# Cross-covariance attention: the output written in rows of 4 KB instead of 2 KB, with 16 output matmuls a group instead of 8

## The chip, the core and the metric

The kernel runs on one core of a Trainium2 chip. The metric is the device time of one execution, in microseconds (us). A core has a matrix engine (TensorE; the profile calls its matmuls PE and its weight loads PEld), VectorE (DVE), ScalarE (ACT), GpSimd (POOL) and SyncE, whose queue (SPq) issues nearly all transfers here. 16 DMA engines move data between HBM and the on-chip memory SBUF; matmuls write to PSUM, which only PE, DVE and ACT reach.

## The reference

Q, K and V are float32 of 8 batches x 12 heads x 512 rows x 64 columns. Attention here is over the 64 columns, not the rows:

```python
Q_norm = Q / (np.linalg.norm(Q, axis=-2, keepdims=True) + 1e-10)
K_norm = K / (np.linalg.norm(K, axis=-2, keepdims=True) + 1e-10)
attn = np.einsum('bhnd,bhne->bhde', Q_norm, K_norm)
attn = np.exp(attn - np.max(attn, axis=-1, keepdims=True))
attn = attn / (np.sum(attn, axis=-1, keepdims=True) + 1e-10)
return np.einsum('bhnd,bhde->bhne', V, attn)
```

So each of 96 heads has a 64 x 64 matrix of column products, a softmax over it, and one multiplication of V by it. Inputs are 37.7 MB, the output is 12.6 MB.

## The kernel before

**Units.** Four heads make a unit u (24 of them, `HU = 4`), two units a pair s (12, `S`), two pairs a group w (6, `W`). A tile has 128 partitions: 32 partitions for each of the four heads of a unit, and in each partition `T = 16` consecutive rows of 64 columns, 4 KB of float32.

**Stages of a pair.** `load_qk` brings Q and K (lines 180 to 184), `load_v` brings V (lines 191 and 193). `cast_qk` (line 204, DVE) makes bfloat16 of them side by side. `grams` (line 224, PE) multiplies: 64 weight loads and 64 matmuls a unit, four heads at a time in four row strips of 32 of the array; unit 23, the last (`WIDE`), takes 32 in strips of 64. `squares` (line 231) and `sums` (line 243) on DVE take the norms, `cross` copies the products of Q and K out of PSUM, `powers` and `scales_q` (lines 249 to 262, ACT) make the scales, `scale_k` (line 254, POOL) applies K's, `logits` (line 267, PE) transposes, `exps` (line 273, ACT) takes the exponentials with their sums, and `normalise` (lines 279 and 282, DVE) writes them as bfloat16 into a tile `ab`.

**V and the output.** `cast_v` (lines 167 and 169) makes bfloat16 of V, `vtrans` (line 293, PE) transposes it in pieces of 8 transposes, `vcopy` (lines 165 and 167) takes a piece to SBUF as `vt`. `outs` (line 310, PE) multiplies `vt`, as weights, with `ab`, one group x = 0 to 3 of a pair at a time: 8 weight loads and 8 matmuls, each of 64 output partitions, into a PSUM tile `po` of 128 x 512 float32, of which there are two (`ps_o`, `bufs=2`). `ocopy` (lines 165 and 167) copies a `po` to a part of a tile `so`; it has 13 buffers of 4 KB a partition. Two groups fill one `so`, and `store` (line 198) writes it: 512 KB, in HBM rows of 2 KB. The very last `so` goes in two stores of 256 KB.

**The order of work.** It is laid down before the launch. `Order` (line 22) is a planner: it holds pieces of work with an engine, a cost, what each must come after, and a rank, and deals them out on a clock of its own. Each engine then works in that fixed order. The DMA queue is one of its engines: SPq issues loads and stores in the planned order, and each issue waits for the eighth issue before it to have landed and for what its buffer needs. Rotating buffers bind the stages: Q and K are three pairs deep, V three half groups, `qkb` two units, `vt` two groups.

The planner also has a rule for PE's own instructions. It counts weight loads and matmuls, and lets the count pass 190, and each further 256, only 6.1 us after the last such passage:

```python
CHUNK, FETCH, FIRST = 256, 6.1, 190
```

Lines 342 to 345 give it the number of instructions in a piece: 128 for a unit's grams, 16 for a piece of `vtrans`, 16 for a group of `outs`.

Of the kernel before, what the change touches and what calls it, by code (L numbers as in the profile page):

```python
# [13 lines left out]
D = 64  # L14
T = 16
HU = 4
J = T // 2
LN_EXP = 6
LO, HI = slice(0, D), slice(D, 2 * D)

# [82 lines left out]
def kernel(  # L103
# [27 lines left out]
    Qw = Q.rearrange("b h (p j) d -> (b h p j d)", j=J).rearrange("(u m p x) -> u p m x", m=2, p=128, x=J * D)  # L131
    Kw = K.rearrange("b h (p j) d -> (b h p j d)", j=J).rearrange("(u m p x) -> u p m x", m=2, p=128, x=J * D)

    Of = out.rearrange("b h n d -> (b h n d)").rearrange(
        "(w r e i p x) -> w e i p r x", r=2, e=2, i=2, p=128, x=J * D)

    ctx.enter_context(tc.manual_schedule())

    NB = dict(qk=3, v=3, vb=2, qkb=2, vt=2, so=13, sm=2, ab=4)
    const = ctx.enter_context(tc.tile_pool(name="const", bufs=1))  # L140
    qp = ctx.enter_context(tc.tile_pool(name="qp", bufs=NB["qk"]))
    vp = ctx.enter_context(tc.tile_pool(name="vp", bufs=NB["v"]))
# [49 lines left out]
        else:  # L192
            nc.sync.dma_start(out=o[:, c], in_=i[:, c])

    def store(s, i, k=None):
        rows = slice(None) if k is None else slice(k * (J // 2), (k + 1) * (J // 2))
        o = Of[s // 2, s % 2, i].rearrange("p r (j d) -> p r j d", d=D)
        nc.sync.dma_start(out=o[:, :, rows], in_=so[s, i][:, :, rows])

    def cast_qk(u, x):  # L200
        s, r = divmod(u, 2)
# [83 lines left out]

    def vtrans(w, q, f):

        js = range(2 * q, 2 * q + 2) if f is None else (2 * q + f,)
        pool = ps_v if f is None else late_pool()
        ps = vps[w, q, f] = pool.tile([128, 4, len(js), 128], BF16, name="vps")  # L290
        for n, j in enumerate(js):
            for c in range(4):
                nc.tensor.transpose(ps[:, c, n, :], vb[w][:, J * c + j].rearrange("p r d -> p (r d)"), identb)  # L293

    def vcopy(eng, w, q, f):
        if w not in vt:
            vt[w] = vtp.tile([128, J, 128, 4], BF16, name="vt")
        o = vt[w][:, 2 * q:2 * q + 2] if f is None else vt[w][:, 2 * q + f:2 * q + f + 1]
        copy(eng, o, vps[w, q, f].rearrange("p c j x -> p j x c"))

    def outs(s, x):
        i, k = divmod(x, 2)
        w, half = divmod(s, 2)
        po[s, x] = ps_o.tile([128, J // 2, 2, D], F32, name="po")
        for j in range(J // 2):
            for e in range(2):
                h = 2 * i + e
                x16 = slice(16 * (4 * half + h), 16 * (4 * half + h + 1))
                v = vt[w][:, k * (J // 2) + j, x16, :].rearrange("p x c -> p (x c)")
                nc.tensor.matmul(po[s, x][e * D:(e + 1) * D, j].rearrange("p r d -> p (r d)"), v, ab[s][:, h, :])  # L310

    def ocopy(eng, s, x):
        i, k = divmod(x, 2)
        if k == 0:
            so[s, i] = sop.tile([128, 2, J, D], F32, name="so")
        o = so[s, i][:, :, k * (J // 2):(k + 1) * (J // 2)].rearrange("p r j d -> p j r d")
        copy(eng, o, po[s, x])


# [22 lines left out]
    def size(key):  # L342
        if key[0] == "gr" and key[1] >= WIDE:
            return 64
        return 8 if key[0] == "vt" and key[-1] is not None else {"gr": 128, "lg": 8, "vt": 16, "ou": 16}[key[0]]

    plan = Order(size)
    X = 1.29
# [4 lines left out]
    def v_at(v):  # L353
        return V_FROM + V_PACE * v / U

    def piece(key, engines, after, behind, rank, fn, *args):
        if key[0] in ("cv", "vc", "oc", "kq", "sc"):
            plan.add(key, engines, after, behind, rank, lambda eng: fn(eng, *args))
        else:
            plan.add(key, engines, after, behind, rank, lambda eng: fn(*args))  # L360
# [39 lines left out]
    def turns(w):  # L400
        return [(q, f) for q in range(4) for f in ((0, 1) if w == W - 1 and q >= TAIL else (None,))]
# [28 lines left out]
            piece(("vc", w, q, f), copies, [("vt", w, q, f)] + free, [("vc", w, *turns(w)[n - 1])] if n else [], R["vc"] + 0.02 * w, vcopy, w, q, f)  # L430
    for s in range(S):
        for x in range(4):
            i, k = divmod(x, 2)
            n = 4 * s + x - 2
            wait = [("oc", n // 4, n % 4)] if n >= 0 else []
            order = [("ou", s, x - 1) if x else back("ou", s, 1, 3)]
            piece(("ou", s, x), {"PE": 0.5}, [("vc", s // 2, *t) for t in turns(s // 2) if t[0] // 2 == k] + [("nm", s)] + wait, order, R["ou"] + 0.01 * s, outs, s, x)
            n = 2 * s + i - NB["so"]
            free = [("st", n // 2, n % 2)] if k == 0 and n >= 0 else []
            order = [("oc", s, x - 1) if x else back("oc", s, 1, 3)]  # L440
            piece(("oc", s, x), {"ACT": 0.6, "DVE": (0.68, BIAS["oc"])} if s >= BOTH else {"ACT": 0.6}, [("ou", s, x)] + free, order, R["oc"] + 0.01 * s, ocopy, s, x)
        for i in range(2):
            order = [("st", s, 0) if i else back("st", s, 1, 1)]
            if (s, i) == (S - 1, 1):

                piece(("sh", s, i), {"DMA": 0.67}, [("oc", s, 2)], order, v_at(2 * s + i) + ST_LAG, store, s, i, 0)
                piece(("st", s, i), {"DMA": 0.67}, [("oc", s, 3)], [("sh", s, i)], v_at(2 * s + i) + ST_LAG, store, s, i, 1)
            else:
                piece(("st", s, i), {"DMA": X}, [("oc", s, 2 * i), ("oc", s, 2 * i + 1)], order, v_at(2 * s + i) + ST_LAG, store, s, i)

    held, passed = [], False
    for (emit, eng), (_, _, key, _) in zip(plan.run(), plan.order):
# [38 lines left out]
```

## Time and profile before

| | |
|---|---|
| time, median of 3 runs | 129.83 us (129.27 to 129.84) |
| span of the profiled execution, first to last instruction | 127.34 us |
| median less that span | 2.49 us |
| PE matmuls: busy, count | 76.9 us, 2128 |
| DVE, ACT, POOL busy | 93.0, 72.5, 39.0 us |
| mean rate of all DMA over the span | 398 GB/s |
| last instruction but the end of the program: the last store's issue | 117.80 us |

The page gives the profiled execution by its span; its own time with what lies around the span is taken as the span and the 2.49 us above. A line of the timeline or of the groups reads: start and length (or busy time), engine, line of the kernel, operation, output tile <- input tiles, number of instructions; in square brackets, how long the engine stood idle before it and what ended that. "issue" there means that no wait which the profile shows ended the idle time. A row of the table by stage gives a stretch, its length, each engine's busy time in it with the number of instructions, the granted clock of PE as a share, the busy share of the DMA engines, and GB/s.

### The profile page before, as it was taken

To read this page: it belongs to the slowest core of one execution; us is meant where nothing else is said; L and a number is where in the kernel's file an instruction comes from. 1 tells how busy PE (TensorE), PEld (TensorE's weight loads), DVE (VectorE), ACT (ScalarE), POOL (GpSimd) and SP (SyncE) were. 2 spreads that over 40 slices of the span, in tenths; PEclk is the share of its full clock that TensorE was granted. 3 is DMA by queue.
4 is the path that set the end of the run, shared out by engine and by line. 5 is a ranking of instruction groups with operands and counts; after the bars stand their busy time and mean duration, and the time that the engine had idled before them with its cause. 6 is when DMAs were issued, how large, how long until landed. Compare 5 with 4: busy or idle time off the path is not lost.

```text
span 127.3 us, 4886 instructions
## 1 busy us (share of the span) xinstructions
PE 76.9 (60%) x2128; PEld 63.2 (50%) x2128; DVE 93.0 (73%) x141; ACT 72.5 (57%) x220; POOL 39.0 (31%) x40
## 2 busy tenths in 40 slices
PE   0055292695946187976982999586857895647000
PEld 0045281584736075854871767374646683535000
DVE  3443749909799959997799999996999969970000
ACT  4000430737988008878395579877564799988000
POOL 4004417120834900432074301502670663300000
PEclk9999999559996555798699599968997799995555
DMA  4999999999999999999999999999999999999993
GB/s 151 353 425 409 422 414 417 417 426 414 425 423 419 408 421 413 414 419 416 430 413 415 412 422 421 417 432 416 404 405 419 399 402 401 405 402 404 409 368 109
DMA packets 15893, 50.66 MB, mean 398 GB/s; under 512 B 1408, under 2 KB 1920, under 8 KB 14464
## 3 DMA queue, kind: packets, MB, share of 16 engines
q1 hardware_dynamic: 15584, 50.34, 98.4%
q8 instruction: 16, 0.26, 0.7%
q10 hardware_dynamic: 288, 0.02, 0.2%
q14 instruction: 5, 0.04, 0.1%
HBM read 37.77 MB, written 12.58 MB: 395 GB/s over the span
## 4 chain that ended last, share of the span: by engine, by line
DVE 45%; PE 22%; issue 9%; ACT 8%; DMA 5%; SPq 1%; POOL 1%; DVEq 0%; ACTq 0%
DVE qkb L204 21%; PE gram L224 13%; DVE scr L231 9%; DVE ab L282 6%; DMA qk<-in_K_dram 5%; PE vps L293 5%; DVE vt L167 4%; PE po L310 4%; ACT ex L273 3%; DVE n L243 2%; ACT so L165 2%; ACT vt L165 2%; DVE vb L167 2%; PE lg L267 1%; DVE so L167 1%
## 5 line engine op out<-in xcount | busy, mean ns | idle before, releaser
L224 PE MATMUL gram<-qkb 32*128 32x128 bf16 (+1 forms) x1504 | 36.5, 263 | 22.9 <-DVE qkb L204 11.6
L204 DVE CAST qkb<-qk 128x1024 bf16<-128x1024 f32 x48 | 40.6, 870 | 7.4 <-DMA qk<-in_Q_dram 4.3
L224 PEld LDWEIGHTS <-qkb 32*128 32x128 bf16 (+1 forms) x1504 | 31.1, 118 | 27.1 <-DVE qkb L204 14.0
L169 POOL TENSOR_SCALAR vb<-v 128x1024 bf16<-128x1024 f32 x19 | 23.9, 1270 | 30.3 <-DMA v<-in_V_dram 24.1
L165 ACT COPY so<-po 128x512 f32<-128x512 f32 x45 | 24.9, 594 | 5.1 <-PE po L310 4.9
L165 ACT COPY vt<-vps 128x1024 bf16<-128x1024 bf16 (+1 forms) x18 | 17.8, 987 | 17.1 <-PE vps L293 17.0
L254 POOL TENSOR_TENSOR kqs<-kq,r 64x512 f32<-64x512 f32 x12 | 13.8, 1152 | 41.3 <-issue 23.1
L293 PE MATMUL vps<-identb,vb 128*128 128x128 bf16 x192 | 18.4, 249 | 8.2 <-DVE vt L167 3.8
L310 PE MATMUL po<-ab,vt 128*64 128x128 bf16 x384 | 19.3, 239 | 6.2 <-issue 2.5
L231 DVE SCALAR_TENSOR_TENSOR scr<-gram,eye 64x512 f32<-64x512 f32 x24 | 16.5, 688 | 7.7 <-PE gram L224 7.3
L293 PEld LDWEIGHTS <-vb 128*128 128x128 bf16 x192 | 13.8, 111 | 11.5 <-issue 6.4
L310 PEld LDWEIGHTS <-vt 128*64 128x64 bf16 x384 | 13.7, 119 | 10.4 <-issue 5.1
L273 ACT ACTIVATE ex<-lg,rq 128x64 f32<-128x64 f32 x48 | 14.5, 322 | 2.8 <-PE lg L267 2.8
L165 ACT COPY kq<-gram 64x512 f32<-64x512 f32 x12 | 7.0, 581 | 14.4 <-DVE scr L231 14.2
L282 DVE TENSOR_TENSOR ab<-ex,rinv 64x256 bf16<-64x256 f32 x24 | 13.2, 552 | 0.6
L273 ACT ACTIVATION_READ_ACCUMULATOR ex<-lg,rq 128x1 f32 x48 | 10.2, 213 | 0.0
L167 DVE COPY vt<-vps 128x1024 bf16<-128x1024 bf16 (+1 forms) x8 | 7.9, 1021 | 1.2 <-PE vps L293 1.1
L267 PE MATMUL lg<-eye,kqs 64*128 64x64 f32 x48 | 6.5, 262 | 2.9 <-POOL kqs L254 2.5
L243 DVE TENSOR_REDUCE n<-scr 128x8 f32<-128x512 f32 x12 | 8.2, 680 | 0.1
L267 PEld LDWEIGHTS lg<-eye,kqs 64*128 64x128 f32 x48 | 4.6, 161 | 4.7 <-POOL kqs L254 3.0
L249 ACT ACTIVATE ln<-n 128x8 f32<-128x8 f32 x12 | 2.7, 229 | 3.3 <-DVE n L243 3.3
L279 DVE RECIPROCAL rinv<-esum 128x4 f32<-128x4 f32 x12 | 2.1, 173 | 3.2 <-ACT ex L273 3.2
(17 smaller groups left out, 17.4 us busy)
## 6 DMA issues: line engine op xcount, KB each, us to landing
out_dram<-so SPq DMA_DIRECT2D x23, 512.0 KB, 10.2
v<-in_V_dram SPq DMA_DIRECT2D x11, 1024.0 KB, 17.5
qk<-in_Q_dram SPq DMA_DIRECT2D x8, 1024.0 KB, 15.9
qk<-in_K_dram SPq DMA_DIRECT2D x8, 1024.0 KB, 18.0
qk<-in_Q_dram SPq DMA_DIRECT2D x8, 512.0 KB, 11.5
qk<-in_K_dram SPq DMA_DIRECT2D x8, 512.0 KB, 11.3
v<-in_V_dram SPq DMA_DIRECT2D x2, 512.0 KB, 10.7
out_dram<-so SPq DMA_DIRECT2D x2, 256.0 KB, 8.6
```

Of the source, the lines that this page charges most:

```text
L165: nc.scalar.copy(o, i)
L167: nc.vector.tensor_copy(o, i)
L169: nc.gpsimd.tensor_scalar(out=o, in0=i, scalar1=1.0, scalar2=0.0, op0=ALU.mult, op1=ALU.add)
L204: nc.vector.tensor_copy(qkb[u][:, :, x * D:(x + 1) * D], qk32[s][:, x, r])
L224: nc.tensor.matmul(gram[s][:, h, r, 0], x, x, start=(t == 0), stop=(t == (T if u < WIDE else J) - 1))
L231: nc.vector.scalar_tensor_tensor(out=scr[s][half], in0=gram[s][half, :, :, 0, half].rearrange("p h r d -> p (h r) d"), scalar=1e-20, in1=e ...
L254: (nc.vector if eng == "DVE" else nc.gpsimd).tensor_tensor(out=kqs[s][HI], in0=kq[s][HI], in1=r8[s][HI, :, None].to_broadcast([D, 2 * HU, ...
L267: nc.tensor.transpose(l[:, h, :], kqs[s][HI, 2 * h:2 * h + 2].rearrange("p r d -> p (r d)"), eye2[HI])
L273: nc.scalar.activation(e[:, h, :], lg[s][:, h, :], AF.Exp, scale=rq[s][:, h:h + 1], accum_out=z[:, h:h + 1])
L282: nc.vector.tensor_tensor(out=a[half, :, half], in0=e[half], in1=ri[half, :, None].to_broadcast([D, HU, D]), op=ALU.mult,)
L293: nc.tensor.transpose(ps[:, c, n, :], vb[w][:, J * c + j].rearrange("p r d -> p (r d)"), identb)
L310: nc.tensor.matmul(po[s, x][e * D:(e + 1) * D, j].rearrange("p r d -> p (r d)"), v, ab[s][:, h, :])
```

## The change

A `so` tile now holds all 16 rows of a partition for both units of a pair: 8 KB a partition, 7 buffers instead of 13. All four heads of a unit lie in the 128 partitions as they lie in HBM, so a store of one pair is 1 MB in rows of 4 KB; the last pair goes in two stores of 512 KB (rows of 2 KB). For that, a group of `outs` covers 4 of the 16 rows and all four heads: 16 weight loads of 32 columns and 16 matmuls with 32 output partitions, in four column strips of the array, where it had 8 of 64 in two strips. There are still 48 groups, each of which fills the same 128 x 512 `po`. `vt` is laid out by 16 rows with two column halves instead of 8 rows with four; a piece of `vtrans` is still 8 transposes and a copy still 1024 elements a partition. A store waits for the four copies of its pair instead of two. The planner is told of 32 instructions in a group instead of 16, 0.6 us of PE instead of 0.5, and DMA pieces of 1 MB; it lays down a new order for all engines.

```diff
--- before.py
+++ after.py
+QT = T // 4
...
-    Of = out.rearrange("b h n d -> (b h n d)").rearrange(
-        "(w r e i p x) -> w e i p r x", r=2, e=2, i=2, p=128, x=J * D)
+    Of = out.rearrange("b h (p t) d -> (b h p) (t d)", t=T).rearrange("(w r e p) x -> w e p r x", r=2, e=2, p=128)
...
-    NB = dict(qk=3, v=3, vb=2, qkb=2, vt=2, so=13, sm=2, ab=4)
+    NB = dict(qk=3, v=3, vb=2, qkb=2, vt=2, so=7, sm=2, ab=4)
...
-    def store(s, i, k=None):
-        rows = slice(None) if k is None else slice(k * (J // 2), (k + 1) * (J // 2))
-        o = Of[s // 2, s % 2, i].rearrange("p r (j d) -> p r j d", d=D)
-        nc.sync.dma_start(out=o[:, :, rows], in_=so[s, i][:, :, rows])
+    def store(s, k=None):
+        o = Of[s // 2, s % 2].rearrange("p r (j d) -> p r j d", d=D)
+        rows = slice(None) if k is None else slice(k * J, (k + 1) * J)
+        nc.sync.dma_start(out=o[:, :, rows], in_=so[s][:, :, rows])
...
-        js = range(2 * q, 2 * q + 2) if f is None else (2 * q + f,)
+        js = range(QT * q, QT * (q + 1)) if f is None else range(QT * q + QT // 2 * f, QT * q + QT // 2 * (f + 1))
         pool = ps_v if f is None else late_pool()
-        ps = vps[w, q, f] = pool.tile([128, 4, len(js), 128], BF16, name="vps")
+        ps = vps[w, q, f] = pool.tile([128, 2, len(js), 128], BF16, name="vps")
         for n, j in enumerate(js):
-            for c in range(4):
-                nc.tensor.transpose(ps[:, c, n, :], vb[w][:, J * c + j].rearrange("p r d -> p (r d)"), identb)
+            for c in range(2):
+                nc.tensor.transpose(ps[:, c, n, :], vb[w][:, T * c + j].rearrange("p r d -> p (r d)"), identb)
...
     def outs(s, x):
-        i, k = divmod(x, 2)
         w, half = divmod(s, 2)
-        po[s, x] = ps_o.tile([128, J // 2, 2, D], F32, name="po")
-        for j in range(J // 2):
-            for e in range(2):
-                h = 2 * i + e
+        po[s, x] = ps_o.tile([128, QT, 2, D], F32, name="po")
+        for j in range(QT):
+            for h in range(HU):
                 x16 = slice(16 * (4 * half + h), 16 * (4 * half + h + 1))
-                v = vt[w][:, k * (J // 2) + j, x16, :].rearrange("p x c -> p (x c)")
-                nc.tensor.matmul(po[s, x][e * D:(e + 1) * D, j].rearrange("p r d -> p (r d)"), v, ab[s][:, h, :])
+                v = vt[w][:, QT * x + j, x16, :].rearrange("p x c -> p (x c)")
+                nc.tensor.matmul(po[s, x][32 * h:32 * (h + 1), j].rearrange("p r d -> p (r d)"), v, ab[s][:, h, :],
+                                 tile_position=(0, 32 * h))
...
     def ocopy(eng, s, x):
-        i, k = divmod(x, 2)
-        if k == 0:
-            so[s, i] = sop.tile([128, 2, J, D], F32, name="so")
-        o = so[s, i][:, :, k * (J // 2):(k + 1) * (J // 2)].rearrange("p r j d -> p j r d")
+        if x == 0:
+            so[s] = sop.tile([128, 2, T, D], F32, name="so")
+        o = so[s][:, :, QT * x:QT * (x + 1)].rearrange("p r j d -> p j r d")
         copy(eng, o, po[s, x])
...
-        return 8 if key[0] == "vt" and key[-1] is not None else {"gr": 128, "lg": 8, "vt": 16, "ou": 16}[key[0]]
+        return 8 if key[0] == "vt" and key[-1] is not None else {"gr": 128, "lg": 8, "vt": 16, "ou": 32}[key[0]]
...
-            piece(("ou", s, x), {"PE": 0.5}, [("vc", s // 2, *t) for t in turns(s // 2) if t[0] // 2 == k] + [("nm", s)] + wait, order, R["ou"] + 0.01 * s, outs, s, x)
+            piece(("ou", s, x), {"PE": 0.6}, [("vc", s // 2, *t) for t in turns(s // 2) if t[0] == x] + [("nm", s)] + wait, order, R["ou"] + 0.01 * s, outs, s, x)
...
+        order = [back("st", s, 1)]
+        if s == S - 1:
+            piece(("sh", s), {"DMA": X}, [("oc", s, 1)], order, v_at(2 * s) + ST_LAG, store, s, 0)
+            piece(("st", s), {"DMA": X}, [("oc", s, 3)], [("sh", s)], v_at(2 * s + 1) + ST_LAG, store, s, 1)
+        else:
+            piece(("st", s), {"DMA": 2 * X}, [("oc", s, 3)], order, v_at(2 * s + 1) + ST_LAG, store, s)
```

More of the change, by code (lines that the diff above doesn't have):

```diff
@@ L295, in vcopy @@
     def vcopy(eng, w, q, f):
         if w not in vt:
[L297 to L298 removed]
+            vt[w] = vtp.tile([128, T, 128, 2], BF16, name="vt")
+        o = vt[w][:, QT * q:QT * (q + 1)] if f is None else vt[w][:, QT * q + QT // 2 * f:QT * q + QT // 2 * (f + 1)]
         copy(eng, o, vps[w, q, f].rearrange("p c j x -> p j x c"))
     def outs(s, x):
[L302 removed]
@@ L432 @@
         for x in range(4):
-            i, k = divmod(x, 2)
             n = 4 * s + x - 2
@@ L436 @@
             order = [("ou", s, x - 1) if x else back("ou", s, 1, 3)]
-            piece(("ou", s, x), {"PE": 0.5}, [("vc", s // 2, *t) for t in turns(s // 2) if t[0] // 2 == k] + [("nm", s)] + wait, order, R["ou"] + 0.01 * s, outs, s, x)
-            n = 2 * s + i - NB["so"]
-            free = [("st", n // 2, n % 2)] if k == 0 and n >= 0 else []
+            piece(("ou", s, x), {"PE": 0.6}, [("vc", s // 2, *t) for t in turns(s // 2) if t[0] == x] + [("nm", s)] + wait, order, R["ou"] + 0.01 * s, outs, s, x)
+            free = [("st", s - NB["so"])] if x == 0 and s >= NB["so"] else []
             order = [("oc", s, x - 1) if x else back("oc", s, 1, 3)]
             piece(("oc", s, x), {"ACT": 0.6, "DVE": (0.68, BIAS["oc"])} if s >= BOTH else {"ACT": 0.6}, [("ou", s, x)] + free, order, R["oc"] + 0.01 * s, ocopy, s, x)
[L442 to L449, printed above, removed]
+        order = [back("st", s, 1)]
[4 more added lines that the diff above has]
+            piece(("st", s), {"DMA": 2 * X}, [("oc", s, 3)], order, v_at(2 * s + 1) + ST_LAG, store, s)
     held, passed = [], False
```

## The prediction

> **What bounds the kernel now.** I read the page's slices first, then the DMA queues, PE in order of time, a table by stage, and the chain that ended last.
>
> ```profile
> PEclk9999999559996555798699599968997799995555
> DMA  4999999999999999999999999999999999999993
> ...
> q1 hardware_dynamic: 15584, 50.34, 98.4%
> q8 instruction: 16, 0.26, 0.7%
> ```
>
> The DMA engines are busy in every slice, to the end: 50.34 MB of data are the first bound. The second stands in the small row: 0.26 MB in 16 packets, 16 KB each, carry instructions. PE runs 2128 weight loads and 2128 matmuls, 4256 instructions; less the 190 of the planner's rule that is 15.9 times 256. PE's own timeline shows what those packets do:
>
> ```profile
> 59.17 0.39 PE L224 MATMUL gram<-qkb 32*128 32x128 bf16 x13 [1.26 <-issue]
> ...
> 83.13 0.35 PE L310 MATMUL po<-ab,vt 128*64 128x128 bf16 x5 [1.62 <-issue]
> ...
> 89.06 0.67 PE L224 MATMUL gram<-qkb 32*128 32x128 bf16 x33 [1.24 <-issue]
> ...
> 94.98 0.39 PE L224 MATMUL gram<-qkb 32*128 32x128 bf16 x13 [1.36 <-issue]
> ...
> 103.48 1.07 PE L224 MATMUL gram<-qkb 64*128 64x128 bf16 x32
> ...
> 107.89 0.45 PE L293 MATMUL vps<-identb,vb 128*128 128x128 bf16 x5 [0.52 <-issue]
> ```
>
> PE halts in the middle of a run of like matmuls and waits for no engine. From 83.13 to 89.06 and from there to 94.98 it runs 128 pairs of weight load and matmul each time, 256 instructions, in 5.92 us: I read this as the price of a block of instructions, which comes no sooner.
>
> ```profile
> core 0: us, PE busy (x) PEld busy (x) DVE busy (x) ACT busy (x) POOL busy (x), PEclk, DMA share, GB/s
> 9.60:59.17 49.57, 31.71 (x927) 26.33 (x928) 39.58 (x58) 27.13 (x86) 17.93 (x15) 0.79 1.02 417
> 59.17:83.13 23.96, 18.42 (x512) 15.11 (x512) 22.04 (x31) 16.72 (x48) 8.55 (x7) 0.86 1.02 419
> 83.13:107.89 24.76, 18.57 (x513) 15.15 (x513) 21.71 (x34) 18.43 (x56) 10.17 (x8) 0.86 1.04 410
> 107.89:117.80 9.91, 6.33 (x113) 4.99 (x113) 5.81 (x12) 8.92 (x32) 1.04 (x1) 0.82 1.05 404
> ```
>
> The two middle rows hold 8 blocks in 48.72 us; at 5.92 they need 47.4. PE is 75 to 77% busy there and yet has 1.3 us left: in this half its instructions limit it as closely as data limit the DMA engines.
>
> ```profile
> 116.70 1.07 ACT so L165 x2
> ...
> out_dram<-so SPq DMA_DIRECT2D x2, 256.0 KB, 8.6
> ```
>
> The last copy ends at 117.77, the last store is issued at 117.80 and lands 8.6 us later, at 126.4, because stores stand in line ahead of it; 0.9 us end the span. In an idle queue the first 512 KB load landed in 3.3 us. So some 5 us of late work would hide behind that line.
>
> **The change, part by part.**
>
> *DMA.* Bytes stay, store packets halve. In the stage with stores alone the rate is 404 GB/s (2 KB rows), in that with nearly only loads of 4 and 8 KB rows 417. At 417 the 12.58 MB take 30.2 us instead of 31.1: -1.0 us, between 0 (stores are slower as stores) and -2.0 (the page's best slices reach 432). Twelve issues fewer on SPq save nothing: it waits most of the time.
>
> *PE's matmul time.* 384 pairs are added. 64 grams in four row strips take 1.07 us at full clock, 17 ns a pair; `po`'s own rows give 29 ns (16 in 0.64 against 8 in 0.41) and, at half clock, 51 (16 in 1.06 against 8 in 0.65). So 6.5 to 20 us over the span; I take 29 ns, from the same operation, 11 us. A block's 5.92 us is 46 ns a pair, so before the last grams this lies under the wait for instructions and costs nothing; were that wait gone, PE's spare time (77% busy) would cover it.
> The Trainium skill, "TensorEngine Tiling (Array Packing)", section Instruction Overhead, gives each matmul a floor of about 60 cycles, an estimated 25 ns at 2.4 GHz, which would be 9.6 us; the grams' 17 ns are under it, so the row decides.
>
> *PE's instructions.* 768 are added, three blocks, 17.8 us of supply. What counts is how many stand ahead of the last grams, which need the last Q and K and start the last softmax. By the instruction lists the last gram is weight load 1984 before and 2220 after: 236 pairs more, 1.84 blocks, 10.9 us. Against it stand reserves: 1.3 us in the two middle rows, and in the first row 7 blocks (from weight load 95, at about 10.5, on) take 48.7 us where 41.4 would do, 7.3 us. Some 4.2 of these lie before the fifth unit's grams end, at 25.64 and 1.85 blocks after load 95 (11.0 us); their place in the list is the same in both kernels and they wait for loads, so 3.1 can be used. The last gram, at 104.55 now, comes 10.9 - 4.4 = 6.5 us later if all reserve is used, 10.9 if none. I take +7.5, 112.05: the new list nearly always has output work ready.
> The Trainium skill, "Runtime: NRT & Kernel Launch", section Instruction fetch mechanics, says that PE's instructions are fetched ahead in 16 KiB blocks of 256, and that the fetch is hidden. The block size agrees with 16 packets of 16 KB; "hidden" does not agree with the 1.24 to 1.62 us halts. By that rule this term would be 0, and the time that of the first or second rival.
>
> *The loads' order.* The last K now stands behind 41.96 MB instead of 39.34 (four stores of 1 MB instead of five of 512 KB, and both halves of the last V). At 418 GB/s that is 6.3 us: issued at 86.98 with 12.5 us to landing, it lands at 99.5 now and at 105.8 then. Cast and grams of its unit follow in about 3 us, so it allows the last gram at 109: under the 112.05, hidden by PE's wait, but near.
>
> *The tail.* From the last gram to the last copy are 13.2 us now, with 13 output groups left. The new list leaves 16, and pair 9's exponentials too. The last 8 groups start at 112.42 and are copied by 117.77, 0.67 us each: three more are +2.0. The exponentials of a pair are 1.3 us of ACT, which the copies also need: +1.3 (0 to 2.3, with DVE's 1.0 to normalise). 16 groups with 8 more pairs at 29 ns are 3.7 us, half of it beside the 0.59 us copies: +1.9 (0 to 6.5, the half-clock row for all). Sum 18.4; last copy at 130.45.
>
> *The end.* Pair 8's store needs a group that in the list follows the last grams, so DMA runs out of stores and idles: the line that now covers 8.6 us is gone. The last store, 512 KB, needs 3.3 us as in an idle queue, and 0.7 for the rest of pair 10's 1 MB, ready some 3 us before it: it lands at 134.45. With the 0.9 us after it the span is 135.35 instead of 127.34: +8.0. DMA's gain of 1.0 is not in this sum, being off the path. The median of the runs lies 2.49 us above the profiled span; I carry this over: 129.83 + 8.0 = **137.8 us**.
>
> *At nothing.* `vtrans` and `vcopy` keep 8 transposes and 1024 elements a copy (ACT 1012 ns, DVE 1225) in another order of reading; I bound that by 0.1 us a copy either way, 2.6 us over 26 copies, hidden by DVE and ACT waits. A store waits for four copies, not two, and SPq holds the next loads behind it; loads are issued 16 to 18 us before they land, which covers it. If it did not, each us of delay would reach the grams. The seven `so` buffers make pair 11's first copy wait for pair 4's store, first in line after the last K: some 15 us early.
>
> **Rivals.**
>
> *DMA stays the bound (faster).* Three more blocks fit in, because the planner plans for them, and the tail hides behind the stores. For it: DMA 9 in every slice and 5 us of cover. Against it: 1.3 us of reserve in the middle rows. Place: the last copy. It decides if that comes before about 122.5, the DMA end of 125.4 less 3 us. Time: 129.83 - 1.0 = 128.8.
>
> *The last K is the bound, not instructions.* If blocks can come faster than 5.92 us when PE needs more, the last gram is at 109. With a tail of 16.5 (2.0 and 1.3 more than now) the last copy is at 125.5, landing with 4.0 at 129.5: +3.1, 132.9. For it: 6.3 us more data ahead. Against it: two equal intervals of 5.92.
>
> *Four column strips do not run beside each other.* Then the half-clock price holds through the tail: 16 groups x 8 x 51 ns, none hidden, 6.5 instead of 1.9, and before the last grams 51 ns exceed the 46 of a block: 137.8 + 4.6 = 142.4, more with the latter. For it: the clock is at half from 115 on (last slices 5). Against it: the four row strips.
>
> **How the numbers follow.** The forecast, instructions with a longer tail, 134.5 to 143: 0.62. Last K: 0.17 (130.5 to 134.5). Column strips slow, or no reserve used, above 143: 0.10. DMA stays the bound: 0.08. No change: 0.03. The range reaches from the last-K case to the top of the forecast: 131 to 143, and holds 0.79. 0.5%, 0.65 us, is about what a measurement of this kernel tells from no change. Faster 0.08, same 0.03, slower 0.89.
>
> **What the profile after would show.** Instructions: 19 packets on the instruction queue, halts on "issue" at equal distances of about 5.9 us over the whole run, last gram near 112, DMA slices under 9 in the last 15 us, the last store landing within 5 us of its issue. Wrong if: DMA is at 9 to the end (first rival); last gram near 109 just after its cast, without halts (second); 16 `po` matmuls take over 0.9 us at full clock (third). The DMA step: a store-only stretch at about 417 GB/s.

## The result, and the profile after

| | before | after |
|---|---|---|
| median of the runs on one chip | 129.55 us (128.97 to 129.84, 4 runs) | 135.56 us (135.18 to 136.17, 4 runs) |
| ratio | | 1.0484, 95% interval 1.0436 to 1.0533 |
| span of the profiled execution | 127.34 us | 133.6 us |
| end of the last gram | 104.55 | 112.17 |
| end of the last copy of an output group | 117.77 | 128.24 |
| last store landed | 126.5 | 132.54 |

The change costs 6.3 us by the ratio. The forecast of 137.8 us is 2.2 us too high: sign, mechanism and range hold, and the size, +8.0 us, is a quarter too large. Three of the kernels in the experiments below scatter by some 5 us from run to run, so ratios leave disturbed runs out throughout.

First the page of the kernel after: the slices, the queues, two groups and the last stores.

```profile
DMA  4999999999999999999999999999999997406894
GB/s 164 333 414 414 430 411 422 412 434 407 436 414 412 421 416 427 405 427 428 416 414 421 422 408 433 421 417 416 416 414 406 416 379 308 183 39 282 359 408 175
...
q1 hardware_dynamic: 12320, 50.34, 92.3%
q8 instruction: 19, 0.31, 0.8%
...
L224 PE MATMUL gram<-qkb 32*128 32x128 bf16 (+1 forms) x1504 | 38.4, 266 | 37.4 <-issue 19.6
...
L308 PE MATMUL po<-ab,vt 128*32 128x128 bf16 x768 | 21.3, 257 | 4.3 <-DVE so L167 1.6
...
out_dram<-so SPq DMA_DIRECT2D x2, 512.0 KB, 4.3
```

After the first slice the DMA engines are at 9 up to the 33rd, and then run down over three (7, 4, 0; 39 GB/s in the slice around 119 us). Before, they were at 9 until the last slice. The instruction queue carries 19 packets of 16 KB instead of 16. The grams have the same count and nearly the same busy time as before, but they stood idle for 19.6 us on "issue", where it had been 3.9 before. 768 output matmuls are busy for 21.3 us; 384 took 19.3. The grams in the kernel before:

```profile
L224 PE MATMUL gram<-qkb 32*128 32x128 bf16 (+1 forms) x1504 | 36.5, 263 | 22.9 <-DVE qkb L204 11.6 <-DVE qk L178 6.2 <-issue 3.9
```

Next, PE in order of time in the kernel after (start, length, line, operation, count; in brackets the idle time before, and what ended it).

```profile
56.65 0.66 PE L224 MATMUL gram<-qkb 32*128 32x128 bf16 x33 [2.76 <-issue]
...
62.58 0.94 PE L224 MATMUL gram<-qkb 32*128 32x128 bf16 x53 [0.96 <-issue]
...
68.77 1.00 PE L224 MATMUL gram<-qkb 32*128 32x128 bf16 x29 [3.54 <-issue]
...
108.76 0.46 PE L224 MATMUL gram<-qkb 32*128 32x128 bf16 x19 [0.33 <-DVE qkb L204]
110.33 1.84 PE L224 MATMUL gram<-qkb 32*128 32x128 bf16 x77 [1.11 <-issue]
...
125.69 1.11 PE L308 MATMUL po<-ab,vt 128*32 128x128 bf16 x32 [0.19 <-ACT so L165]
```

The halts now run through the whole kernel. In the list of DMA packets the instruction packets start at 30.59, 36.55, 42.53 and so on to 108.06: 13 steps of 5.96 us in the mean, where I had 5.92 from two intervals. The halts vary from 0.96 to 3.54 us, because the work in between is a longer or a shorter part of 5.96. The last one falls into the middle of the last grams: 19 of unit 22 run at 108.76, as soon as DVE has cast that unit's K, and its other 45 and the 32 of unit 23 wait 1.11 us more for instructions and end at 112.17. DVE has cast the last K, unit 23's, by 109.91. Without this halt its grams, 1.07 us, could have ended near 111 (an estimate from these rows); the rest of the delay lies further ahead, in grams and casts that come late.

The table by stage shows what is left of the cover at the end (start and end, length, busy time and instructions of PE, PEld, DVE, ACT, POOL, granted clock, DMA share, GB/s).

```profile
core 0: us, PE busy (x) PEld busy (x) DVE busy (x) ACT busy (x) POOL busy (x), PEclk, DMA share, GB/s
30.60:108.10 77.50, 55.07 (x1705) 44.61 (x1699) 66.95 (x94) 45.36 (x136) 27.64 (x22) 0.76 1.02 418
108.10:118.00 9.90, 6.72 (x196) 5.48 (x199) 9.71 (x17) 7.35 (x30) 1.83 (x2) 0.88 0.60 242
118.00:128.30 10.30, 7.32 (x216) 5.15 (x208) 4.27 (x12) 9.34 (x29) 0.25 (x1) 0.67 0.68 275
128.30:133.60 5.30, 0.00 (x0) 0.00 (x0) 0.00 (x0) 0.00 (x0) 0.00 (x0) 0.50 0.67 261
```

For 77.5 us PE is busy 71% of the time and DMA is full at 418 GB/s: two limits at once. From 108 on DMA runs at 60 to 68% because stores wait for copies (those of pairs 7 and 8 are issued at 111.30 and 119.12), and DVE is busy 9.71 of 9.90 us. The last copy ends at 128.24; before, stores stood in line for 8.6 us behind it, now the last one lands 4.3 us after its issue.

In spans: last gram +7.62 us, from there to the last copy 16.07 instead of 13.22 (+2.85), from the last copy to the end 5.36 instead of 9.57 (-4.21). The sum is the 6.26 us between the spans.

### The profile page after: what moved, and what is told of

Read it like the earlier page. It is cut to its first block, busy times and chain, and to the rows that moved or that the text cites. A ratio compares the mean times of both kernels' runs of the same rounds, so it can differ in the third digit from the quotient of the medians.

```text
span 133.6 us, 5626 instructions
## 1 busy us (share of the span) xinstructions
PE 83.3 (62%) x2512; PEld 67.2 (50%) x2512; DVE 98.0 (73%) x147; ACT 69.9 (52%) x215; POOL 37.9 (28%) x39
## 3 DMA queue, kind: packets, MB, share of 16 engines
q1 hardware_dynamic: 12320, 50.34, 92.3%
HBM read 37.77 MB, written 12.58 MB: 377 GB/s over the span
## 4 chain that ended last, share of the span: by engine, by line
PE 38%; DVE 24%; issue 14%; DMA 11%; ACT 8%; ACTq 0%
PE gram L224 19%; PE vps L293 11%; DVE qkb L204 10%; DMA qk<-in_K_dram 8%; DVE scr L231 7%; PE po L308 7%; ACT so L165 3%; DVE ab L282 3%; ACT ex L273 3%; DMA first<-in_Q_dram 3%; PE lg L267 2%; DVE vt L167 2%; DVE so L167 2%; ACT vt L165 1%; DVE n L243 1%
## 5 line engine op out<-in xcount | busy, mean ns | idle before, releaser
L224 PE MATMUL gram<-qkb 32*128 32x128 bf16 (+1 forms) x1504 | 38.4, 266 | 37.4 <-issue 19.6
L165 ACT COPY vt<-vps 128x1024 bf16<-128x1024 bf16 (+1 forms) x16 | 15.8, 988 | 24.8 <-PE vps L293 24.7
L165 ACT COPY so<-po 128x512 f32<-128x512 f32 x42 | 23.5, 597 | 6.2 <-PE po L308 6.1
L308 PE MATMUL po<-ab,vt 128*32 128x128 bf16 x768 | 21.3, 257 | 4.3 <-DVE so L167 1.6
L231 DVE SCALAR_TENSOR_TENSOR scr<-gram,eye 64x512 f32<-64x512 f32 x24 | 16.5, 688 | 9.5 <-PE gram L224 9.3
L293 PE MATMUL vps<-identb,vb 128*128 128x128 bf16 x192 | 20.6, 272 | 2.3 <-POOL vb L169 1.2
L308 PEld LDWEIGHTS <-vt 128*32 128x32 bf16 x768 | 14.6, 111 | 9.3 <-issue 6.2
L293 PEld LDWEIGHTS <-vb 128*128 128x128 bf16 x192 | 15.6, 122 | 5.7 <-issue 2.4
L282 DVE TENSOR_TENSOR ab<-ex,rinv 64x256 bf16<-64x256 f32 x24 | 11.9, 495 | 0.6
L167 DVE COPY vt<-vps 128x1024 bf16<-128x1024 bf16 (+1 forms) x10 | 10.4, 1060 | 0.1
L167 DVE CAST vb<-v 128x1024 bf16<-128x1024 f32 x6 | 5.5, 912 | 2.1 <-DMA v<-in_V_dram 2.1
```

The costliest lines, as they stand in the source:

```text
L165: nc.scalar.copy(o, i)
L167: nc.vector.tensor_copy(o, i)
L224: nc.tensor.matmul(gram[s][:, h, r, 0], x, x, start=(t == 0), stop=(t == (T if u < WIDE else J) - 1))
L231: nc.vector.scalar_tensor_tensor(out=scr[s][half], in0=gram[s][half, :, :, 0, half].rearrange("p h r d -> p (h r) d"), scalar=1e-20, in1=e ...
L282: nc.vector.tensor_tensor(out=a[half, :, half], in0=e[half], in1=ri[half, :, None].to_broadcast([D, HU, D]), op=ALU.mult,)
L293: nc.tensor.transpose(ps[:, c, n, :], vb[w][:, T * c + j].rearrange("p r d -> p (r d)"), identb)
```

## The experiments

**1. The split of the output matmuls alone.** The kernel before, with each output matmul of 64 columns cut in two of 32 in four column strips; groups, order, `vt`, stores and the planner stay.

```diff
-                x16 = slice(16 * (4 * half + h), 16 * (4 * half + h + 1))
-                v = vt[w][:, k * (J // 2) + j, x16, :].rearrange("p x c -> p (x c)")
-                nc.tensor.matmul(po[s, x][e * D:(e + 1) * D, j]..., v, ab[s][:, h, :])
+                for z in range(2):
+                    x8 = slice(16 * (4 * half + h) + 8 * z, 16 * (4 * half + h) + 8 * (z + 1))
+                    v = vt[w][:, k * (J // 2) + j, x8, :].rearrange("p x c -> p (x c)")
+                    q = 32 * (2 * e + z)
+                    nc.tensor.matmul(po[s, x][q:q + 32, j]..., v, ab[s][:, h, :], tile_position=(0, q))
```

> The kernel before with one part of the change: each output matmul of 64 columns is cut into two of 32 in four column strips, 16 pairs a group instead of 8. Layout, stores and the order of all work stay as before. Theory (PE's instructions come in blocks of 256, one per 5.9 us while the DMA engines are busy): 19 instruction packets instead of 16; the last gram moves from weight load 1984 to 2264, 2.19 blocks or 13.0 us, less 4.4 us of reserve: it ends near 113 instead of 104.6, the last copy is near 126, time 132.5 to 134.5. Rival 'loads' order' (the late last K is what costs): the loads are untouched, so no change, 129.6 within 0.7. Rival 'matmul time' (four column strips run one after the other): 16 po matmuls take over 0.9 us at full clock instead of about 0.45.

Measured: 134.29 us (133.41 to 134.84), ratio 1.0404 (1.0344 to 1.0463), which is 5.2 us over its 129.14. PE in order of time in this kernel:

```profile
103.16 0.39 PE L224 MATMUL gram<-qkb 32*128 32x128 bf16 x13 [1.38 <-issue]
...
109.08 1.01 PE L224 MATMUL gram<-qkb 32*128 32x128 bf16 x57 [0.68 <-issue]
...
110.58 1.07 PE L224 MATMUL gram<-qkb 64*128 64x128 bf16 x32
...
115.00 0.29 PE L293 MATMUL vps<-identb,vb 128*128 128x128 bf16 x1 [2.86 <-issue]
```

The last gram ends at 111.65, halts stand 5.92 us apart, and one of 2.86 us falls into the tail. The last K landed as early as in the kernel before, near 99. So 768 more instructions, with order, loads and stores as they were, make most of the loss.

**2. The larger unit of storing alone.** The kernel before with its matmuls of 64 columns, in which the planner has a pair's store come after all four copies, as two transfers of 512 KB in rows of 2 KB.

```diff
-    NB = dict(qk=3, v=3, vb=2, qkb=2, vt=2, so=13, sm=2, ab=4)
+    NB = dict(qk=3, v=3, vb=2, qkb=2, vt=2, so=7, sm=2, ab=4)
...
-    def store(s, i, k=None):
...
+    def store(s, k=None):
...
+        for n in (0, 1) if k is None else (k,):
+            nc.sync.dma_start(out=o[:, n], in_=i[:, n])
...
+            piece(("st", s), {"DMA": 2 * X}, [("oc", s, 3)], order, v_at(2 * s + 1) + ST_LAG, store, s)
```

> The kernel before with the other part of the change: a pair is stored when all four of its groups are copied (two stores of 512 KB issued together, rows still 2 KB; the last pair in two steps), with the planner's DMA pieces of the changed kernel. Output matmuls stay at 8 a group, 2128 pairs, 16 instruction packets. Eight stores of 512 KB now stand before the last K instead of five, and the last V after it: 40.9 MB instead of 39.3, so it lands some 3.8 us later, near 103. Theory (instruction blocks): the last gram is near 106.5, the last copy near 120, stores still stand in line then, time 129.5 to 131. Rival 'loads' order': most of the loss is here, 132.5 or more.

Four runs gave 128.84, 130.84, 131.31 and 132.55, too far apart for a verdict, so the same kernel ran again in more rounds.

> The kernel before with its matmuls of 64 columns, in which a pair's output is stored when all four groups are copied, as two stores of 512 KB in rows of 2 KB together, in the planned order of the larger stores; the same kernel as the run whose times spread from 128.84 to 132.55. Theory (the larger unit of storing is a small part of the loss, the instructions are the large one): median 129 to 131 us, at most a third of the 6.3 us. Rival (half or more of the loss): over 132 us.

Measured: median 130.70 (128.98 to 133.85, 12 runs), ratio 1.0066 (1.0022 to 1.0109): 0.9 us. Its trace shows that this kernel did not quite do what I meant. In the tail the two stores of a pair went 1.31 us apart, because each waits only for the two copies that it reads. The third version cuts a pair's stores by unit, so that each needs all four copies.

```diff
-        for n in (0, 1) if k is None else (k,):
-            nc.sync.dma_start(out=o[:, n], in_=i[:, n])
+        if k is None:
+            for r in (0, 1):
+                nc.sync.dma_start(out=o[:, :, r], in_=i[:, :, r])
+        else:
+            nc.sync.dma_start(out=o[:, k], in_=i[:, k])
```

> As the run with the larger unit of storing alone (matmuls of 64 columns), but the two stores of a pair are cut by unit and not by pair of heads, so that each needs all four copies of its pair; 512 KB each, rows of 2 KB as before. In the run before it the first of the two stores left 1.31 us ahead of the second in the tail, as soon as its own two copies had ended (issues at 122.34, 123.66, 124.97), and the last store landed 2.70 us after its issue. Theory (waiting for four copies costs in the tail alone: pair 10's 1 MB leaves at once, 1.3 us later for its first half, so the last 512 KB finds 1.3 us more of stores ahead and lands about 4.0 after its issue, as in the kernel after with 4.3): 1.0 to 1.6 us over that run's 130.4 in its undisturbed runs, 131.2 to 132.2. Rival (the wait for four copies is free, as the prediction had it): within 0.6 us of 130.4.

Measured: median 131.16 (129.28 to 134.65, 12 runs), ratio 1.0099 (1.0059 to 1.0140): 1.3 us. The wait itself shows as expected: the last store lands 4.11 us after its issue instead of 2.70. The time does not: the medians behind the two ratios are 130.65 and, in the version before, 130.35, and the intervals of the two ratios overlap. The theory's 131.2 was too much and the rival's range holds; the wait for four copies costs at most some tenths, and these runs do not tell it from nothing. Single runs of both versions reach some 134 us, which no trace here explains.

One more thing in the second version's trace matters. PE in order of time:

```profile
108.31 1.01 PE L294 MATMUL vps<-identb,vb 128*128 128x128 bf16 x8 [2.03 <-DVE vt L167]
109.25 1.89 PE L225 MATMUL gram<-qkb 64*128 64x128 bf16 x32
```

Its last gram ends at 111.14, within half a microsecond of experiment 1, and yet its profiled span is 3.8 us shorter (128.6 against 132.4). Tail and end make the difference: 13.8 us from last gram to last copy against 15.3 (where the halt of 2.86 lies), and 2.7 us for the last store against 4.6. The expectation had put its last gram near 106.5 and its last copy near 120; they came at 111.14 and 125, so the time fell into the range for another reason than was given. Instructions are not the reason: there are 16 packets, PE does not halt on issue after 98.09, and ahead of the last grams it waits 2.03 us for a DVE copy of `vt`. In the third version the last gram ends at 108.84. So the planned order with larger stores makes the last gram late by itself, by 4.3 to 6.6 us, and the time is then about 1 us longer. A late last gram is not the loss by itself. It becomes one with a longer tail behind it, and in experiment 1 the instructions make both.

The split alone (5.2, interval 4.4 to 6.0) and the larger unit (1.3, interval 0.8 to 1.8) sum to 6.5 us; both together are 6.3.

**3. Fewer grams: is it the instructions ahead of the last gram?** The kernel after, with 12 of 16 rows summed in the grams of units 0 to 22.

```diff
-        for t in range(T if u < WIDE else J):
+        last = 3 * T // 4 if u < WIDE else J
+        for t in range(last):
...
```

> The changed kernel with a quarter of the grams left out (12 of the 16 rows of a partition are summed in units 0 to 22, so the softmax is of other numbers); the order of all work and all transfers stay. 368 pairs fewer: 2144, about as many as before the change. Theory (instruction blocks): 16 packets; the last gram waits only for the last K (landing near 106) and ends near 109 instead of 112.2; the last copy is near 125, time 131 to 133. Rival 'loads' order': the loads come as in the changed kernel and the grams were waiting for them anyway: 135.6 within 0.8.

Measured: 132.98 us (132.43 to 133.85), ratio 1.0315 (1.0265 to 1.0366). PE in order of time:

```profile
105.86 0.85 PE L225 MATMUL gram<-qkb 32*128 32x128 bf16 x48 [0.62 <-DVE qkb L204]
107.06 1.07 PE L225 MATMUL gram<-qkb 64*128 64x128 bf16 x32 [0.35 <-DVE qkb L204]
```

No halt on issue is left in this stretch. The last gram ends at 108.13, 4.0 us earlier, and now waits for DVE's cast of a last K that landed at 105.54. By the two ratios 2.2 of the 4.0 us reach the time; the tail behind the last gram is 17.2 us here, where it was 16.07. The prediction's second rival gave the last K 109 and 132.9 us. That limit exists, just behind the first.

**4. Two stores after the last K: is it the loads' order?** The kernel after, with the stores of pairs 2 and 3 issued after the last K. All engines keep their order but SPq.

```diff
+        if key in (("st", 2), ("st", 3)):
+            late_st.append(emit)
+            continue
         emit(eng)
+        if key == ("lk", S - 1, 1):
+            for put in late_st:
+                put("DMA")
```

> The changed kernel with the stores of pairs 2 and 3 issued after the last K instead of before; each engine's order of work stays. The last K stands behind 39.9 MB instead of 42.0 and lands near 101 instead of 106. Theory (instruction blocks): PE is held by its blocks, so the last gram stays near 112 and the last copy near 128; DMA has 2 MB more in line for the idle stretch near 115 to 119, but the last stores still wait for the last copies: 135.6 within 0.8. Rival 'loads' order': the last gram follows K to near 107 to 108, time 131 to 132.5.

Measured: 135.63 us (134.99 to 136.26), ratio 1.0515 (1.0468 to 1.0561): nothing gained. PE in order of time:

```profile
108.74 0.46 PE L224 MATMUL gram<-qkb 32*128 32x128 bf16 x19 [0.20 <-ACT kq L165]
110.41 1.84 PE L224 MATMUL gram<-qkb 32*128 32x128 bf16 x77 [1.21 <-issue]
```

The last K landed 4.7 us earlier, at 101.39, and the last gram still ended at 112.25 after the same halt in the same place. Alone, the order of the loads moves nothing.

**5. Both.** Experiments 3 and 4 in one kernel.

> The changed kernel with both reliefs together: a quarter of the grams left out (as in the earlier run, so the softmax is of other numbers) and the stores of pairs 2 and 3 after the last K. Alone the first gave 133.0 and the second 135.6 us. Theory (instruction blocks first, the last K second): with few enough instructions the earlier K (landing near 101) now counts: the last gram ends near 105, the last copy near 121.5, and DMA has stores in line nearly to the end: 128.5 to 130. Rival 'the longer tail alone' (what is left after the blocks is the 16 groups behind the last gram): no more than 1 us better than 133.0.

Measured: 129.50 us (129.18 to 131.19), ratio 1.0040 (1.0005 to 1.0075). PE in order of time:

```profile
104.37 1.07 PE L225 MATMUL gram<-qkb 64*128 64x128 bf16 x32 [0.35 <-DVE qkb L204]
```

The last gram ends at 105.44, 0.9 us after that of the kernel before, and of the 6.3 us 0.5 are left. Instructions hold the last gram at 112, the last K at 108; with both moved, the loss is gone. It is gone in a kernel that does less work than the kernel before; whether it goes with all work kept is experiment 6. This kernel also shows the rate of stores in rows of 4 KB: only stores ran from 101 to 112 us.

```profile
101.00:112.00 11.00, 7.16 (x203) 6.04 (x200) 10.77 (x19) 8.26 (x31) 1.43 (x2) 0.85 1.02 414
```

It is 414 GB/s, where rows of 2 KB had 404.

**6. The same with all work kept.** Units in strips of 64, as unit 23 has them, need 32 pairs instead of 64, but Q and K in rows of 2 KB. The first version did this for units 16 to 23, with late stores, and the planner planned anew.

```diff
-    WIDE = U - 1
+    WIDE = U - 8
...
-        return (0, 1) if s < ONE or s == S - 1 else (None,)
+        return (0, 1) if s < ONE or 2 * s + 1 >= WIDE else (None,)
```

> All work is kept. The changed kernel with units 16 to 23 (instead of 23 alone) loaded in rows of 2 KB and multiplied in row strips of 64, 32 pairs a unit instead of 64, and the stores of pairs 2 and 3 after the last K; the planner lays the order anew. 2288 pairs, the last gram at weight load 1988, as before the change. Theory: 18 instruction packets at most, the last gram near 105, the last copy near 121, time 128.5 to 130: the gain of the 4 KB stores (1 us) and the loss from 2 KB loads (about 0.4) nearly cancel against the kernel before. Rival 'the order of the changed kernel is worse for another reason than instructions': above 132.

Measured: 133.67 us (132.48 to 134.54), ratio 1.0324 (1.0256 to 1.0391): a miss. In the profiled execution, the longest of the four (134.54), the last K landed near 99.3, but the last gram ended at 109.84, after waiting 2.87 us for DVE's cast, which stood behind other work on DVE in the new order. The rival's "above 132" holds; that the order on DVE is the reason was not tested by itself. A version with the same edit for units 20 to 23 was also a miss.

> All work is kept. As the run with units 16 to 23 in strips of 64, but units 20 to 23 alone: 2412 pairs, the last gram at weight load 2124, 0.75 of a block less than in the changed kernel (2220) and 1.06 blocks more than with eight units (1988). Theory: the last gram is at least 13 blocks of 5.96 us after load 351 at about 25.5, plus 0.9 of a block: near 108, the last copy near 124, time 131 to 132.5, between the changed kernel and the run with eight units. Rival: no dependence on the count, equal to the run with eight units within 0.8.

It gave 137.55 us (135.64 to 138.42). Beyond what the expectation says, it left out one store of 1 MB (its queue carries 49.29 MB instead of 50.34), which I had not meant; I draw nothing from it. The next two kept the order of the kernel after on every engine and gave SPq two transfers of 512 KB in the place of one.

```diff
+    WIDE = U - 8        # U - 16 in the second
+    NARROW = U - 1      # what the planner is told
-            nc.sync.dma_start(out=qk32[s][:, x, r]..., in_=(Qw, Kw)[x][U - 1])
+            for i in (0, 1) if r is None else (r,):
+                nc.sync.dma_start(out=qk32[s][:, x, i]..., in_=(Qw, Kw)[x][4 * w + 2 * i + e])
```

> The kernel after, all its work kept, with the stores of pairs 2 and 3 issued after the last K, and units 16 to 22 as well as 23 in strips of 64 (32 pairs of weight load and matmul a unit instead of 64; Q and K of these units come in rows of 2 KB, as two transfers of 512 KB for one of 1 MB). Unlike in the run that let the planner plan anew, every engine keeps the order of the kernel after. 2288 pairs; the last gram is at weight load 1996 instead of 2220 (1984 in the kernel before). Theory (blocks of instructions and the last K each hold the last gram; both are taken away): last K lands near 101, last gram near 105.5 as in the run with a quarter of the grams left out and late stores (105.44), 129.5 to 131.0 us. Rival (the miss of the planned-anew run at 133.67 came from the strips of 64 or the 2 KB loads themselves, not from the new order on DVE): 133 to 134.5 us.

Measured: 133.82 us median, but from 130.93 to 135.70 with no ratio to be given. The lowest run lies inside the theory's range, the median inside the rival's; it settles nothing.

> As the run with units 16 to 23 in strips of 64, with units 8 to 23 in strips of 64: 2032 pairs, last gram at weight load 1740, so 1.9 blocks (some 11 us at 5.96) fewer ahead of the last gram than with units 16 to 23. Theory: with 2288 pairs the instructions are no longer the bound, the last K is; more pairs taken away bring nothing, and 8 MB more in rows of 2 KB cost up to 0.65 us (404 against 417 GB/s): 129.5 to 131.5 us, within 1 us of the run with units 16 to 23. Rival (instructions still hold the last gram there): 1.5 us or more faster than that run.

Measured: 132.16 us (131.66 to 132.86, 6 runs), ratio 1.0230 (1.0179 to 1.0280): 0.7 us over the theory's range. Against the run with units 16 to 23 it is 1.7 us below the median and 1.2 above the lowest, so that comparison, on which theory and rival were to part, stays open. PE in order of time:

```profile
104.11 2.27 PE L226 MATMUL gram<-qkb 64*128 64x128 bf16 x64 [0.62 <-DVE qkb L206]
```

No halt on issue is left near the end, and the last gram ends at 106.38, 5.8 us earlier than in the kernel after; that much of the theory holds with all work kept. Yet 3.0 of the 6.3 us of loss remain. Against experiment 5 its span is 2.5 us longer: 0.9 of it before the last gram, which DVE's cast releases, and 1.8 in the landing of the last store, 5.76 us after its issue. Most parts of that store had landed by 127.48, the last one at 129.40; an instruction packet moved from 125.13 to 126.06. That it delayed that part is read from the order of events and was not tested; in experiment 4 the last store took 5.45 us with no instruction packet beside it. So the second half of the loss with all work kept has no shown cause. None of these versions beats the kernel before.

**7. What a block of instructions costs.** PE alone, in one execution: 23 blocks of 128 pairs of weight load and matmul in a row without waits between them, except one early. From about 30 to 95 us the DMA engines carry 12 loads of 1 MB (rows of 4 KB) and then 24 stores of 512 KB (rows of 2 KB); before and after that nothing.

```diff
+    pairs(0, P0)                      # P0 = 128 * 8
+    nc.vector.tensor_copy(tiles[0][:, 0, :128], acc[:, 3, :128])
+    pairs(P0, ALL)                    # ALL = 128 * 23
+    for i in range(12):
+        nc.sync.dma_start(out=tiles[i], in_=Qr[i])
+    for i in range(24):
+        nc.sync.dma_start(out=Or[i], in_=tiles[i // 2][:, :, 512 * (i % 2):512 * (i % 2) + 512])
```

> PE alone, on constant data, nothing of the reference: 23 blocks of 128 pairs of weight load and matmul in four row strips, without any wait but one copy. For the first 8 blocks no DMA runs; then 12 loads of 1 MB (4 KB rows) and 24 stores of 512 KB (2 KB rows), about 60 us, then none again. Theory A (an instruction packet waits behind the data in its DMA engine): 128 pairs take about 3.3 us without traffic and 5.9 us with it, for 4 KB rows as for 2 KB rows. Theory B (the packet has a fixed round trip): 5.9 us throughout. Theory C (it waits behind a fixed number of packets): the stretch with 2 KB rows is shorter by about 1.5 us a block than that with 4 KB rows.

Its PE in order of time, and below it the table by stage, without and with traffic:

```profile
9.71 1.97 PE L43 MATMUL acc<-x 32*128 32x128 bf16 x128 [1.49 <-issue]
13.44 1.97 PE L43 MATMUL acc<-x 32*128 32x128 bf16 x128 [1.76 <-issue]
...
30.98 1.97 PE L43 MATMUL acc<-x 32*128 32x128 bf16 x128 [0.90 <-issue]
37.18 3.60 PE L43 MATMUL acc<-x 32*128 32x128 bf16 x128 [4.23 <-issue]
43.92 3.60 PE L43 MATMUL acc<-x 32*128 32x128 bf16 x128 [3.14 <-issue]
50.12 3.60 PE L43 MATMUL acc<-x 32*128 32x128 bf16 x128 [2.60 <-issue]
...
81.92 3.60 PE L43 MATMUL acc<-x 32*128 32x128 bf16 x128 [3.73 <-issue]
88.66 2.87 PE L43 MATMUL acc<-x 32*128 32x128 bf16 x128 [3.14 <-issue]
95.68 3.60 PE L43 MATMUL acc<-x 32*128 32x128 bf16 x128 [4.15 <-issue]
99.69 1.98 PE L43 MATMUL acc<-x 32*128 32x128 bf16 x128 [0.40 <-issue]
103.41 1.97 PE L43 MATMUL acc<-x 32*128 32x128 bf16 x128 [1.75 <-issue]
```

```profile
core 0: us, PE busy (x) PEld busy (x) DVE busy (x) POOL busy (x), PEclk, DMA share, GB/s
5.00:30.00 25.00, 14.72 (x955) 13.42 (x944) 0.29 (x1) 0.00 (x0) 1.00 0.05 7
35.00:60.00 25.00, 14.41 (x512) 13.61 (x512) 0.00 (x0) 0.00 (x0) 0.50 1.03 409
65.00:85.00 20.00, 10.38 (x420) 9.81 (x411) 0.00 (x0) 0.00 (x0) 0.67 1.05 403
```

A block starts every 3.45 to 3.73 us with the DMA engines empty, every 6.2 to 6.7 under loads, every 6.2 to 7.0 under stores, and again every 3.5 to 3.7 when they are done. So theory B falls, and C too, since rows of 2 KB are no quicker; A's two levels are there, both somewhat higher than it said. The packet itself takes 0.9 to 1.2 us in either case, and a block starts 2.2 to 2.7 us after its packet does (7.38 to 9.71, 34.81 to 37.18); so nearly all of the 2.7 us more lie ahead of the packet. That it waits there behind data is the reading that fits; the trace does not show where it waits. The half clock under traffic does not explain it. The block at 30.98 runs at full clock (1.97 us), and with the loads under way the next comes only 6.20 us later; the block at 95.68 runs at half clock (3.60 us), the traffic over, and the next comes 4.01 us later. The kernel after shows the same on its own: packets 5.96 us apart while DMA is full, and, as it runs down, at 113.24 and 116.47, 5.18 and 3.23 us after the one before; in the last of these steps the DMA engines are 55% busy. So the rival with faster blocks falls before 108 us, where DMA is full, and blocks hurt the tail there little: the one that starts at 115.53 comes just as PE gets a copy of DVE that it also waits for.

## Why the prediction was right

*DMA.* Predicted -1.0 us, off the path. Experiment 5's stretch gives 414 against 404 GB/s: 12.58 MB in 30.4 instead of 31.1 us, -0.7, and off the path, since DMA runs down over three slices before the end.

*PE's matmul time.* Predicted 29 ns for an added pair, hidden. It is hidden, but it is less: the `po` rows grew by 2.0 us for 384 pairs, 5 ns, below the 17 I had named as the lower end. All PE rows together grew by 83.3 - 76.9 = 6.4 us; the other 4.4 stand in rows whose count is unchanged (grams 1.9, `vtrans` 2.2, logits the rest), and no run here separates why. In the tail a group of 16 takes what a group of 8 took: two groups 1.11 us at half clock, 1.11 and 1.12 before. The third rival wanted over 0.9 us for 16 at full clock; they take 0.41 (at 31.20, for one). The Trainium skill, "TensorEngine Tiling (Array Packing)", section Instruction Overhead, has about 60 cycles for each matmul; 32 `po` matmuls in 0.63 us, 20 ns each, are under the 25 ns estimated from it, as the grams were.

*PE's instructions.* Right, and the largest step: halts 5.96 us apart (5.92) over the whole run, 19 packets, the last gram at 112.17 (112.05). That the last gram agrees to 0.1 us is partly luck: +7.5 was chosen between 6.5 and 10.9, and the larger stores by themselves make it late too (experiment 2). Experiment 1 shows that the instructions cost 5.2 us alone, experiment 3 shows the last gram moving when they are fewer. What was too simple is "comes no sooner": the interval is that of full DMA engines. The Trainium skill, "Runtime: NRT & Kernel Launch", section Instruction fetch mechanics, calls the fetch of the next block mostly hidden; the halts of experiment 7, 1.49 us with empty and 2.6 with full DMA engines, say otherwise for a stream of matmuls this dense.

*The loads' order.* Last K predicted at 105.8, landed at 106.12; predicted hidden but near: 109 against 112. Experiments 3 and 4 show both halves of that, the last gram at 108.13 without the instructions' limit and no gain from an earlier K with it.

*The tail.* Predicted 18.4 us from last gram to last copy, measured 16.07. The term that was mis-sized is the +1.9 for 8 more pairs in 16 groups at 29 ns, half hidden: by the rows above it is about nothing. Without it the sum is 16.5. The three further groups at 0.67 are there: the last nine copies fill 122.39 to 128.24, 0.65 us each. The exponentials of pair 9 are there too, with three logits pieces behind the last gram (113.94, 118.38, 120.55) where there were two (106.64, 111.28); their 1.3 us were not measured by themselves.

*The end.* DMA ran empty as predicted; the last store lands 4.3 us after its issue (4.0), and 1.06 us follow (0.9).

*Around the span.* I carried 2.49 us over; the median of after lies 1.96 above its profiled span. So the 2.2 us of error are -2.3 from the tail, +0.1 from the last gram, +0.5 from the end and -0.5 from here.

*At nothing.* `vtrans` and `vcopy` cost no more: a copy of 1024 takes 1014 ns on ACT and 1221 on DVE, 1012 and 1225 before. The wait for four copies is nearly free in the time (experiment 2, 0.3 us between the two versions), though it delays the last landing by 1.4 us.

*The rivals.* DMA did not stay the bound; with the larger unit alone, without the instructions, the loss is 0.7% (1.0066), though there too DMA falls to between 5 and 8 tenths in three slices near the end. The last K is the next limit, with 132.98 us for the rival's 132.9; its last gram came at 108.13 instead of 109 and its tail took 17.2 us instead of 16.5, so that the sum agrees is partly luck. The column strips run beside each other.

## What to carry to other kernels

Count instructions as a resource beside bytes and busy time: here a block of 128 pairs came no faster than about every 6 us while the DMA engines were full, so PE at 71% busy was nonetheless at its limit, and halving the size of one kind of matmul cost 4% although the matmuls ran no longer. Look for halts on "issue" inside runs of like instructions, at equal distances, and count how many instructions stand ahead of the last work that the end depends on. When two limits stand close together, remove each alone and then both: the runs with one removed gave 133.0 and 135.6 us, that with both 129.5.

## What the runs showed of the hardware that I had not expected

The price of a block depends on data traffic, 3.45 to 3.73 us without and 6.2 to 7.0 with it (experiment 7): its packet starts later, and does not move more slowly. Sixteen matmuls in four column strips take the same 0.41 us at full clock as eight in two. And the last gram can end 6.6 us later than in the kernel before (111.14) with 0.9 us lost, in a kernel whose tail behind it is 13.8 us and whose last store lands 2.7 us after its issue.
